# The mixer's output projection as seven block products, in a two-layer encoder trunk

## The chip, the cores and the metric

The kernel runs on one core of a Trainium2 chip, in one launch. The metric is the device time of one execution in microseconds, the lower the better. All arithmetic is float32 in accuracy: each float32 operand of a matmul is split into a high part, rounded by a copy to the type `F32R`, and a low part, the difference, and each product is three matmuls (high x high, high x low, low x high).

## The reference

Sequence 512, model width 1024, two layers. In each layer:

```
u = RMSNorm(h)
q_a,k_a,v_a, q_r,k_r,v_r,g_r, gate_a,gate_b = split(u @ w_in)
A = dilated attention(q_a,k_a,v_a);  B = silu(g_r) * GroupNorm(retention(q_r,k_r,v_r))
merged = sigmoid(gate_a) * (A @ w_att_out) + sigmoid(gate_b) * (B @ w_ret_out)
h = h + RMSNorm(merged @ w_out)                                  # the mixer's output projection
h = h + RMSNorm(relu(RMSNorm(h) @ w_up)^2 @ w_down)              # the MLP, 4096 wide
h = h + sigmoid(RMSNorm(h) @ w_ple_gate) * RMSNorm(p @ w_ple_proj)
```

The change concerns `merged @ w_out`, a product of 512 x 1024 by 1024 x 1024, and the read-out of `p @ w_ple_proj`.

## The kernel before

**Order of the work.** Only TensorE's (PE's) order is written out by hand. The instructions of the other engines and queues are ordered at build time by a scheduler, by priority and by when they are ready; what is wrapped in `soon` gets 300 steps of priority, so read-outs and norms go ahead of weight splits.

**Weights.** All weights come from one packed array in chunks of 128 x 1024, in the order of `PLAN_LAYER`. `ITEMS` lists what PE uses one after the other: a chunk, or a sum of chunks. `load` (L247) fetches chunks by an SP DMA into the ring `R` of four buffers; `total` (L260) makes a sum in a buffer of ring `X` (two buffers): an SP DMA fetches one chunk, and an accumulating DMA, issued by POOL, adds another. A "chain" adds a further chunk to the sum that product P5 left. `prefetch` (L271) makes the two parts of each item: ACT's copy (L278) for the high one, a subtraction on DVE or POOL (L301) for the low one, into one of five `wt` buffers. `chunk` (L289) asks for an item and runs up to three items ahead.

**Seven products in the MLP.** The down projection already runs six of its eight slices as block products of the Strassen-Winograd kind: `operands` (L826) forms differences of blocks of the activations, `total` differences and sums of weight blocks (signs are folded into additions and the read-outs), `product` (L843) runs one of the seven products, and `evac_prod` (L855) adds it up.

**Around the change.** For c in 0..7, `b_gate` and a matmul job on `ro` run on PE (24 matmuls each), DVE forms `m` (L751), and POOL adds it to `fb` (L752). `fb` holds `merged` transposed, two column groups to a tile. Its eight groups are split into the operand store `uT` (L755). Then `row_job` (L332) runs the output projection ("wo") as two halves of the columns: 96 matmuls for all four token blocks together, then 96 for one token block after the other. `evac_wo` (L761) reads a result out: ACT's sum of squares (L351), DVE's product with the gain (L766), and after the second half `pre_norm` (L393): root on POOL (L359, L361), update of the residual `h` (L773), sums of squares, root, normalised row `un` (L406). Its transposes (L413) and the split into `uT` (L416, L417) are put off by seven steps of PE work, or eight in what follows (`step`, `pending`).

Then "pp", the ple projection, takes 48 matmuls, its operands `phl` and two weight chunks whose low parts POOL makes (`POOL_MORE`); its read-outs alternate between ACT (L794) and DVE (L796). The first three chunks of the MLP's "up" run early, the columns of token blocks 0 and 1 first, then those of blocks 2 and 3 (L862 to L875).

PSUM has eight banks: `acc` (four), `s` (two) and `tp` (two), each a ring.

Of the kernel before, what the change touches and what calls it, by code (L numbers as in the profile page):

```python
# [28 lines left out]
PRIO = 300  # L29
POOL_MORE = [("pp",0),("pp",1)]  # L30
BG = 40
# [31 lines left out]
def _slot(e):  # L63
# [16 lines left out]
    + [("gb", c) for c in range(GB)] + [x for c in range(8) for x in ([("gb", c)] if c >= GB else []) + [("ro", c)]]  # L80
    + [("wo", c) for c in range(8)]
    + [("pp", c) for c in range(2)]
# [10 lines left out]
def _items():  # L93
    out = []
    for i in range(NL):
        for kind, c in PLAN_LAYER:
            e = 2 * (c // 8) + c % 4 // 2
            if kind == "up" and c >= 4 and c // 4 <= UNITS:
# [101 lines left out]
def block(ctx: ExitStack, tc: tile.TileContext, x, pT, w, dl, gains, cs, lc, rel, eye, out):  # L200
# [58 lines left out]

    def total(key, src):  # L260
        if src[0] == "chain":
            r = chain["sum"]
        else:
            r = blk("X", [P, D], name="wsum")
            nc.sync.dma_start(r, rows(src[0]))
            if key[1] == "P5":
                chain["sum"] = r
        nc.gpsimd.dma_start(r, rows(src[1]), accum_op=ALU.add)  # L268
        return r
# [369 lines left out]
    def one_layer(i, h):  # L639
# [106 lines left out]
        for c in range(8):  # L746
# [5 lines left out]
            nc.gpsimd.tensor_tensor(fb[c // 2][:, c % 2, :], m, fb[c // 2][:, c % 2, :], op=ALU.add)  # L752
        for c in range(8):
            src = fb[c // 2][:, c % 2, :]
            split(uT[:, :, c, :], src)  # L755
        g_post, g_pre = gain_row(5 * i + 1), gain_row(5 * i + 2)

        acc = [blk("V", [P, D], name="acc") for _ in range(NT)]
        ssq = [[None, None] for _ in range(NT)]

        def evac_wo(hf):  # L761
            @soon
            def f(t, ps):
                hs_ = HALVES[hf]
                ssq[t][hf] = sumsq(ps, t2("junk"), None if hf else 1e-6)
                nc.vector.tensor_tensor(acc[t][:, hs_], ps, g_post[:, hs_], op=ALU.mult)  # L766
                if hf:
                    pre_norm(h[t], t, g_pre, residual(t, acc, rstd_of(*ssq[t])))
            return f

# [4 lines left out]

        row_job([(i, "wo", c) for c in range(4)], u_lhs, evac_wo(0))
        row_job([(i, "wo", 4 + c) for c in range(4)], u_lhs, evac_wo(1), ONES)

# [7 lines left out]
        for hf in range(2):  # L786
            hsl = slice(hf * S, (hf + 1) * S)
            ch = chunk(i, "pp", hf)
            for t in range(NT):
                ps = bank(PP_BANKS[4 * hf + t])  # L790
                for k in range(2):
                    row_mm(ps, ch, k, lambda a, k, t: phl[k][:, a, t * P:(t + 1) * P], k, t, k == 0, k == 1)
                if t % 2:
                    nc.scalar.activation(pn[t][:, hsl], ps, AF.Copy)  # L794
                else:
                    nc.vector.tensor_copy(pn[t][:, hsl], ps)  # L796
                step(AGE_PP)
# [64 lines left out]
        early = []  # L862
        for j in range(2):
            settle(PAIRS[j])
            for c in range(EARLY):
                if not j:
                    early.append(bank(EARLY_BANKS[c]))
# [169 lines left out]
```

## Time and profile before

| | us |
|---|---|
| Time, median of 3 runs | 1796.14 (1793.64 to 1797.11) |
| Profiled execution, its own time | 1794.64 |
| Its span, first to last instruction | 1792.9 |
| Mean granted clock of TensorE | 1.0 of full speed |

| Engine | busy us | share |
|---|---|---|
| PE, matmuls | 1772.4 | 99% |
| PE, weight loads | 1466.2 | 82% |
| DVE | 1145.4 | 64% |
| ACT | 807.5 | 45% |
| POOL | 382.6 | 21% |

Busy time is the union of an engine's instructions in the profiled execution; the matmuls are pipelined, so that they overlap and their ends are modelled. The DMA queues moved 274.58 MB, 153 GB/s on average.

### The profile page before, as it was taken

Reading aid. Unit: us, or ns where it says so; the run is one execution under the profiler, and the core shown is the slowest. Engines: PE = TensorE matmul, PEld = TensorE weight load, DVE = VectorE, ACT = ScalarE, POOL = GpSimd, SP = SyncE. Lnnn points to the kernel's source line nnn. Section 1 sums busy time; section 2 is a strip of 40 time slices with the busy share of each in tenths; the row PEclk is TensorE's granted clock in tenths of the full one; section 3 lists DMA queues with packets and bytes.
Section 4 is the critical chain, followed back from the end, with each engine's and each line's share of the span. In section 5 each row is a group of like instructions: output and inputs, shape, how many; then the busy total and the mean of one; then the engine's idle time right before and its main releaser. Section 6 shows DMA issues by size and latency. Waiting matters only on the chain.

```text
span 1792.9 us, 22127 instructions
## 1 busy us (share of the span) xinstructions
PE 1772.4 (99%) x8209; PEld 1466.2 (82%) x8209; DVE 1145.4 (64%) x1803; ACT 807.5 (45%) x1271; POOL 382.6 (21%) x354
## 2 busy tenths in 40 slices
PE   8999999999999999999999999999999999999998
PEld 6888788888898888888788887888888888888887
DVE  6676777743465677674656767677444657667754
ACT  4255444332466454433443555444333664444342
POOL 2312244311142001002123222442012410000030
PEclk9999999999999999999999999999999999999999
DMA  5555464552347655552346545555422566664421
GB/s 213 194 193 159 149 212 137 166 175 95 117 142 188 165 158 161 156 184 70 129 141 214 165 145 172 184 159 187 136 101 99 165 170 156 169 175 130 165 71 60
DMA packets 87807, 274.58 MB, mean 153 GB/s; under 512 B 11921, under 2 KB 20497, under 8 KB 87698
## 3 DMA queue, kind: packets, MB, share of 16 engines
q1 hardware_dynamic: 80786, 247.99, 40.7%
q0 software_dynamic: 6912, 25.17, 8.3%
q8 instruction: 65, 1.06, 0.2%
q14 instruction: 44, 0.36, 0.1%
HBM read 239.55 MB, written 33.55 MB: 152 GB/s over the span
## 4 chain that ended last, share of the span: by engine, by line
PE 89%; DVE 4%; POOL 2%; ACT 2%; issue 1%; DMA 1%; SPq 0%; POOLq 0%; ACTq 0%
PE acc L312 28%; PE acc L322 19%; PE s L312 18%; PE acc L849 8%; PE tp L849 4%; PE tp L612 2%; PE tp L544 2%; PE tp L507 2%; PE acc L871 1%; PE tp L413 1%; POOL wt L301 1%; PE s L525 1%; PE s L526 1%; PE s L590 1%; PE s L871 1%
## 5 line engine op out<-in xcount | busy, mean ns | idle before, releaser
L312 PE MATMUL acc<-uT,wt 128*128 128x512 f32 x1920 | 472.8, 392 | 0.0
L312 PEld LDWEIGHTS acc<-uT,wt 128*128 128x128 f32 x1920 | 356.2, 188 | 71.8
L301 DVE TENSOR_TENSOR wt<-raw,wt 128x1024 fp32r<-128x1024 f32 x217 | 279.4, 1292 | 187.6 <-ACT wt L278 187.1
L278 ACT ACTIVATE wt<-raw 128x1024 fp32r<-128x1024 f32 x280 | 293.9, 1055 | 223.0 <-PE acc L312 114.0
L322 PE MATMUL acc<-wt,uT 128*128 128x512 f32 x1320 | 320.8, 396 | 4.4 <-ACT uT L416 1.8
L312 PE MATMUL s<-uT,wt 128*128 128x512 f32 x1392 | 323.7, 389 | 0.0
L312 PEld LDWEIGHTS s<-uT,wt 128*128 128x128 f32 x1392 | 261.1, 188 | 54.1
L322 PEld LDWEIGHTS acc<-wt,uT 128*128 128x128 f32 x1320 | 245.6, 189 | 55.6 <-DVE uT L417 2.6
L301 POOL TENSOR_TENSOR wt<-raw,wt 128x512 fp32r<-128x512 f32 x126 | 173.2, 1395 | 408.1 <-ACT wt L278 339.1
L849 PE MATMUL acc<-wt,op 128*128 128x512 f32 x672 | 159.5, 389 | 0.0
L849 PEld LDWEIGHTS acc<-wt,op 128*128 128x128 f32 x672 | 126.1, 188 | 26.2
L268 POOL DMA_DIRECT2D wsum<-in_w_dram x48 | 42.8, 900 | 420.1 <-DVE wt L301 141.0
L892 ACT ACTIVATE relu<-s 128x512 f32<-128x512 f32 x60 | 35.7, 595 | 180.7 <-PE s L312 172.0
L860 DVE TENSOR_TENSOR sumP<-acc,sumP 128x512 f32<-128x512 f32 x92 | 61.8, 686 | 56.4 <-PE acc L849 56.1
L312 PE MATMUL acc<-retT,wt 128*128 128x512 f32 x384 | 89.3, 389 | 0.0
L322 PE MATMUL acc<-wt,ff 128*128 128x512 f32 x384 | 88.5, 390 | 0.0
L301 DVE TENSOR_TENSOR wt<-wsum,wt 128x1024 fp32r<-128x1024 f32 x48 | 60.6, 1263 | 41.7 <-ACT wt L278 41.7
L312 PEld LDWEIGHTS acc<-retT,wt 128*128 128x128 f32 x384 | 72.1, 188 | 15.0
L322 PEld LDWEIGHTS acc<-wt,ff 128*128 128x128 f32 x384 | 71.8, 188 | 14.8
L304 ACT ACTIVATE rt<-rz 128x512 fp32r<-128x512 f32 x64 | 40.3, 631 | 91.5 <-DVE rz L594 91.0
L849 PE MATMUL tp<-wt,op 128*128 128x512 f32 x336 | 80.7, 389 | 0.0
L849 PEld LDWEIGHTS tp<-wt,op 128*128 128x128 f32 x336 | 63.1, 188 | 13.1
(165 smaller groups left out, 2153.5 us busy)
## 6 DMA issues: line engine op xcount, KB each, us to landing
raw<-in_w_dram SPq DMA_DIRECT2D x280, 512.0 KB, 3.7
wsum<-in_w_dram POOLq DMA_DIRECT2D x48, 512.0 KB, 5.5
kk<-stk SPq DMA_DIRECT2D x128, 128.0 KB, 3.8
wsum<-in_w_dram SPq DMA_DIRECT2D x24, 512.0 KB, 3.3
stq<-rr SPq DMA_DIRECT2D x16, 512.0 KB, 3.4
qs<-stq SPq DMA_DIRECT2D x128, 64.0 KB, 2.9
stk<-rr SPq DMA_DIRECT2D x16, 512.0 KB, 3.0
stv<-vr SPq DMA_DIRECT2D x16, 512.0 KB, 4.4
```

The source lines that it names most:

```text
L268: nc.gpsimd.dma_start(r, rows(src[1]), accum_op=ALU.add)
L278: nc.scalar.activation(t[:, 0, :], r, AF.Copy)
L301: eng.tensor_tensor(dst, src, hi.bitcast(F32), op=ALU.subtract)
L304: nc.scalar.activation(dst[:, 0], src, AF.Copy, scale=scale)
L312: nc.tensor.matmul(ps, lhsT=t[:, a, (off + k) * P:(off + k + 1) * P], rhs=r, start=k == 0 and n == 0, stop=k == kts - 1 and n == 2)
L322: nc.tensor.matmul(ps, lhsT=lhs(a, k, t), rhs=ch[:, b, j * S:(j + 1) * S], start=first and n == 0, stop=last and n == 2)
L507: nc.tensor.matmul(o, lhsT=v, rhs=pt[k][:, hl, :], start=k == 0 and hl == 0, stop=k == 3 and hl == 1)
L544: nc.tensor.transpose(ps[:, t * P:(t + 1) * P], zs[t][:, k * P:(k + 1) * P], ident)
L612: nc.tensor.matmul(o, lhsT=v[:, k, a * P:(a + 1) * P], rhs=rt[k][:, b, :], start=n == 0, stop=n == 11)
L849: nc.tensor.matmul(ps, lhsT=op[:, a, k, j * P:(j + 1) * P], rhs=t[:, b, k * S:(k + 1) * S], start=k == 0 and n == 0, stop=k == 1 and n == 2)
L860: nc.vector.tensor_tensor(a, ps, a, op=ALU.add)
L871: nc.tensor.matmul(early[c][:, 256 * j:256 * j + 256], lhsT=t[:, a, k * P:(k + 1) * P], rhs=uT[:, b, k, 256 * j:256 * j + 256], start=k == ...
```

## The change

`w_out` and `merged` are cut into two by two blocks: tokens in halves of 256, the inner dimension and the columns in halves of 512. Seven products P1 to P7 replace the eight block products; each has two weight items (q = 0, 1) of 12 matmuls. P5 and P7 use a sum of two weight chunks, P6 and P4 add one more chunk to P5's sum, which is held in ring `X`; P7's sum goes into ring `R`. The operands are differences of blocks of `fb`; P1, P5, P4 and P2 keep theirs in `uT`, the others in new tiles of ring `P`. The results of a product are read out by DVE additions into `acc`; P4 finishes token blocks 2 and 3, P2 blocks 0 and 1, and the early "up" takes blocks 2 and 3 first. Gain products of the right halves go to POOL. The low parts of pp's two weight chunks move from POOL to DVE, and its read-outs all go to ACT, with priority.

```diff
-POOL_MORE = [("pp",0),("pp",1)]
+POOL_MORE = []
...
-    + [("wo", c) for c in range(8)]
+    + [("wo", c) for c in (0, 1, 4, 5, 6, 7, 2, 3)]
...
+                if c == 0:
+                    b11, b21, b12, b22 = ([CHUNK[i, "wo", 2 * b + q] for q in range(2)] for b in range(4))
+                    out += [((i, "wo" + p, q), tuple(b if b == "chain" else b[q] for b in src)) for p, src in (
+                        ("P1", (b11,)), ("P5", (b11, b12)), ("P6", ("chain", b22)), ("P7", (b12, b22)),
+                        ("P3", (b22,)), ("P4", ("chain", b21)), ("P2", (b21,))) for q in range(2)]
+                continue
...
     def total(key, src):
+        at = key[2] if key[1][:2] == "wo" else "sum"
         if src[0] == "chain":
-            r = chain["sum"]
+            r = chain[at]
         else:
-            r = blk("X", [P, D], name="wsum")
+            held = key[1][-2:] == "P5"
+            r = blk("X" if held or at == "sum" else "R", [P, D], name="wsum")
             nc.sync.dma_start(r, rows(src[0]))
-            if key[1] == "P5":
-                chain["sum"] = r
+            if held:
+                chain[at] = r
         nc.gpsimd.dma_start(r, rows(src[1]), accum_op=ALU.add)
...
-        for c in range(8):
-            src = fb[c // 2][:, c % 2, :]
-            split(uT[:, :, c, :], src)
...
+        def wo_operand(x, q, src, at=None):
+            if at is None:
+                at = blk("P", [P, 2, 2, 256], F32R, name="wop")
+            nc.scalar.activation(at[:, 0], src, AF.Copy)
+            nc.vector.tensor_tensor(at[:, 1], src, at[:, 0].bitcast(F32), op=ALU.subtract)
+            wop[x, q] = at
...
+        def sum_x(q, o):
+            nc.vector.tensor_tensor(o, f2[q][:, :, 256:], f1[q][:, :, 256:], op=ALU.subtract)
+            return o
...
+        for q in range(2):
+            wo_operand("P1", q, f1[q][:, :, :256], lo_k[q][:, :, :, :256])
+        wx = sums(sum_x)
+        wy = sums(sum_y)
+        for q in range(2):
+            wo_operand("P5", q, wx[q], lo_k[q][:, :, :, 256:])
+            wo_operand("P6", q, wy[q])
+        wz = sums(sum_z)
+        for q in range(2):
+            wo_operand("P7", q, wz[q])
+        wv = sums(sum_v)
+        for q in range(2):
+            wo_operand("P3", q, wv[q])
+        for q in range(2):
+            wo_operand("P4", q, f2[q][:, :, 256:], hi_k[q][:, :, :, 256:])
+        for q in range(2):
+            wo_operand("P2", q, f2[q][:, :, :256], hi_k[q][:, :, :, :256])
...
+        def done_wo(t, hf, src, eng):
+            hs_ = HALVES[hf]
+            ssq[t][hf] = sumsq(src, t2("junk"), None if hf else 1e-6)
+            eng.tensor_tensor(acc[t][:, hs_], src, g_post[:, hs_], op=ALU.mult)
+            if not hf:
+                pre_norm(h[t], t, g_pre, residual(t, acc, rstd_of(*ssq[t])))
...
+        @soon
+        def evac_wo(x, j, ps):
+            (l1, r1), (l2, r2) = ([a[:, sl] for sl in HALVES] for a in (acc[j], acc[2 + j]))
+            if x == "P1":
+                nc.scalar.activation(l1, ps, AF.Copy)
+            elif x == "P5":
+                w5.append(ps)
+            elif x == "P6":
+                nc.vector.tensor_tensor(l2, ps, l1, op=add)
+                nc.vector.tensor_tensor(r1, w5[j], l2, op=add)
+            elif x == "P7":
+                nc.vector.scalar_tensor_tensor(r2, ps, -1.0, r1, op0=ALU.mult, op1=ALU.subtract)
+                nc.vector.tensor_tensor(l2, ps, l2, op=add)
+                done_wo(2 + j, 1, r2, nc.gpsimd)
+            elif x == "P3":
+                nc.vector.scalar_tensor_tensor(r1, ps, -1.0, r1, op0=ALU.mult, op1=ALU.subtract)
+                done_wo(j, 1, r1, nc.gpsimd)
+            elif x == "P4":
+                nc.vector.tensor_tensor(l2, ps, l2, op=add)
+                done_wo(2 + j, 0, l2, nc.vector)
+            else:
+                nc.vector.tensor_tensor(l1, ps, l1, op=add)
+                done_wo(j, 0, l1, nc.vector)
+
+        w5 = []
+        wo_banks = [bank(tag) for tag in ("acc", "acc", "s", "s", "acc", "acc")]
+        for m, pr in enumerate(("P1", "P5", "P6", "P7", "P3", "P4", "P2")):
+            pss = [wo_banks[(2 * m + j) % 6] for j in range(2)]
+            for q in range(2):
+                t = chunk(i, "wo" + pr, q)
+                for j in range(2):
+                    for k in range(2):
+                        for n, (a, b) in enumerate(HL):
+                            nc.tensor.matmul(pss[j], lhsT=wop[pr, q][:, a, k, j * P:(j + 1) * P], rhs=t[:, b, k * S:(k + 1) * S],
+                                             start=q == 0 and k == 0 and n == 0, stop=q == 1 and k == 1 and n == 2)
+                    if q:
+                        evac_wo(pr, j, pss[j])
+                    step()
...
-                if t % 2:
-                    nc.scalar.activation(pn[t][:, hsl], ps, AF.Copy)
-                else:
-                    nc.vector.tensor_copy(pn[t][:, hsl], ps)
+                soon(nc.scalar.activation)(pn[t][:, hsl], ps, AF.Copy)
...
-        for j in range(2):
+        for j in (1, 0):
             settle(PAIRS[j])
             for c in range(EARLY):
-                if not j:
+                if j:
                     early.append(bank(EARLY_BANKS[c]))
```

## Rows read from the trace of the kernel before

**Rows 1.** Page, part 1: engine, busy us (share of the span), instructions.

```profile
PE 1772.4 (99%) x8209; PEld 1466.2 (82%) x8209; DVE 1145.4 (64%) x1803; ACT 807.5 (45%) x1271; POOL 382.6 (21%) x354
```

**Rows 2.** Who waited for whom, PE alone: total us, times, longest; first and last of nine.

```profile
PE tp L544 <- DVE pt L301: 3.5, 2, 1.7
...
PE tp L413 <- DVE un L403: 0.7, 2, 0.3
```

**Rows 3.** Timeline of PE, layer 0, output projection to early up: start us, us, operation.

```profile
455.02 5.60 PE L312 MATMUL acc<-retT,wt 128*128 128x512 f32 x24
...
460.46 35.52 PE L322 MATMUL acc<-wt,uT 128*128 128x512 f32 x156
...
518.47 3.04 PE L871 MATMUL s<-uT,wt 128*128 128x256 f32 x24
...
527.11 3.04 PE L871 MATMUL s<-uT,wt 128*128 128x256 f32 x24
```

**Rows 4.** Line 322 in layer 0's output projection: min/median/max ns, first and last start.

```profile
L322 PE MATMUL acc<-wt,uT x192: 387/389/476, 460.5 to 505.6; 128*128 128x512 f32 x192
```

**Rows 5.** Windows: stretch and its length, busy us (instructions) by engine, PE clock, DMA share, GB/s.

```profile
460.50:482.20 21.70, 21.70 (x97) 17.99 (x96) 8.68 (x14) 6.95 (x11) 2.29 (x1) 1.00 0.31 106
482.20:505.80 23.60, 23.60 (x114) 19.68 (x113) 11.80 (x21) 12.23 (x28) 9.84 (x16) 1.00 0.24 90
505.80:518.50 12.70, 12.70 (x66) 10.69 (x65) 12.18 (x18) 7.90 (x16) 1.78 (x5) 1.00 0.70 248
518.50:535.75 17.25, 17.25 (x146) 17.25 (x145) 6.94 (x11) 8.52 (x14) 10.18 (x8) 1.00 0.32 98
...
633.70:677.20 43.50, 43.50 (x193) 36.03 (x192) 30.96 (x40) 20.56 (x27) 4.94 (x6) 1.00 0.63 161
...
1347.10:1405.10 58.00, 58.00 (x273) 48.38 (x272) 32.95 (x52) 27.29 (x55) 13.83 (x21) 1.00 0.37 131
```

**Rows 6.** Groups by line, forms apart: busy us, mean ns, idle before and releaser.

```profile
L278 ACT ACTIVATE wt<-raw 128x1024 fp32r<-128x1024 f32 x280 | 293.9, 1055 | 223.0 <-PE acc L312 114.0 <-PE acc L322 73.1 <-PE acc L849 16.5
...
L301 POOL TENSOR_TENSOR wt<-raw,wt 128x512 fp32r<-128x512 f32 x126 | 173.2, 1395 | 408.1 <-ACT wt L278 339.1 <-DMA kk<-stk 36.0 <-DVE rb L477 19.2
...
L935 POOL TENSOR_TENSOR sumP<-sumP,gain 128x512 f32<-128x512 f32 x8 | 12.1, 1536 | 136.8 <-ACT junk L351 136.8
```

**Rows 7.** Timeline of DVE, layer 0, before and through the output projection and pp.

```profile
450.88 2.12 DVE L301 TENSOR_TENSOR wt<-raw,wt 128x1024 fp32r<-128x1024 f32 x1 [0.34 <-ACT wt L278]
...
492.61 1.41 DVE L406 SCALAR_TENSOR_TENSOR un<-h,rstd,gain 128x512 f32<-128x512 f32 x2 [1.41 <-POOL rstd L361]
...
508.44 1.22 DVE L301 TENSOR_TENSOR wt<-raw,wt 128x1024 fp32r<-128x1024 f32 x1
509.58 0.68 DVE L766 TENSOR_TENSOR acc<-acc,gain 128x512 f32<-128x512 f32 x1
510.18 1.41 DVE L773 SCALAR_TENSOR_TENSOR h<-acc,rstd,h 128x512 f32<-128x512 f32 x2
...
513.78 1.42 DVE L406 SCALAR_TENSOR_TENSOR un<-h,rstd,gain 128x512 f32<-128x512 f32 x2 [0.40 <-POOL rstd L361]
515.12 1.28 DVE L417 TENSOR_TENSOR uT<-tp,uT 128x512 fp32r<-128x512 f32 x2
```

**Rows 8.** Page, part 6: DMA issues of the block sums, KB each, median us to landing.

```profile
wsum<-in_w_dram POOLq DMA_DIRECT2D x48, 512.0 KB, 5.5
...
wsum<-in_w_dram SPq DMA_DIRECT2D x24, 512.0 KB, 3.3
```

**Rows 9.** Timeline of ACT, layer 0: the first square sum of block 0.

```profile
487.86 0.60 ACT L351 ACTIVATE junk<-acc 128x512 f32<-128x512 f32 x1 [3.80 <-PE acc L322]
```

**Rows 10.** Timeline of POOL, layer 0: two additions of the gated branch.

```profile
450.62 1.29 POOL L752 TENSOR_TENSOR fT<-m,fT 128x512 f32<-128x512 f32 x1 [9.59 <-DVE m L751]
461.83 2.29 POOL L752 TENSOR_TENSOR fT<-m,fT 128x512 f32<-128x512 f32 x1 [9.92 <-DVE m L751]
```

More of the change, by code (lines that the diff above doesn't have):

```diff
@@ L97, in _items @@
             e = 2 * (c // 8) + c % 4 // 2
+            if kind == "wo":
+                if c == 0:
[4 more added lines that the diff above has]
+                continue
             if kind == "up" and c >= 4 and c // 4 <= UNITS:
@@ L752, in one_layer @@
             nc.gpsimd.tensor_tensor(fb[c // 2][:, c % 2, :], m, fb[c // 2][:, c % 2, :], op=ALU.add)
-        for c in range(8):
-            src = fb[c // 2][:, c % 2, :]
-            split(uT[:, :, c, :], src)
         g_post, g_pre = gain_row(5 * i + 1), gain_row(5 * i + 2)
+        wop = {}
+        def wo_operand(x, q, src, at=None):
[4 more added lines that the diff above has]
+            wop[x, q] = at
@@ new lines, in one_layer, with sums, sum_z @@
+        f1, f2 = fb[:2], fb[2:]
+        lo_k, hi_k = ([uT[:, :, 4 * kh + 2 * q:4 * kh + 2 * q + 2, :] for q in range(2)] for kh in range(2))
+        def sums(f):
+            return [f(q, t2("ws").rearrange("p (s n) -> p s n", s=2)) for q in range(2)]
+        def sum_x(q, o):
+            nc.vector.tensor_tensor(o, f2[q][:, :, 256:], f1[q][:, :, 256:], op=ALU.subtract)
+            return o
+        def sum_z(q, o):
+            nc.vector.tensor_tensor(o, f1[q][:, :, :256], f1[q][:, :, 256:], op=ALU.subtract)
+            return o
@@ new lines, in sum_y, with sum_v @@
+        def sum_y(q, o):
+            nc.vector.scalar_tensor_tensor(o, wx[q], -1.0, f1[q][:, :, :256], op0=ALU.mult, op1=ALU.subtract)
+            return o
+        def sum_v(q, o):
+            nc.vector.scalar_tensor_tensor(o, wy[q], -1.0, f2[q][:, :, :256], op0=ALU.mult, op1=ALU.subtract)
+            return o
+        for q in range(2):
[5 more added lines that the diff above has]
+            wo_operand("P6", q, wy[q])
@@ L758, in one_layer @@
+        wz = sums(sum_z)
[8 more added lines that the diff above has]
+            wo_operand("P2", q, f2[q][:, :, :256], hi_k[q][:, :, :, :256])
         acc = [blk("V", [P, D], name="acc") for _ in range(NT)]
         ssq = [[None, None] for _ in range(NT)]
[L761 to L769, printed above, removed]
+        LH, RH = HALVES
@@ L774, in residual @@
             return upd
-        row_job([(i, "wo", c) for c in range(4)], u_lhs, evac_wo(0))
-        row_job([(i, "wo", 4 + c) for c in range(4)], u_lhs, evac_wo(1), ONES)
+        def done_wo(t, hf, src, eng):
[4 more added lines that the diff above has]
+                pre_norm(h[t], t, g_pre, residual(t, acc, rstd_of(*ssq[t])))
+        add = ALU.add
```

## The prediction

> **What bounds the kernel now.** I read the busy shares first: TensorE (PE) is busy for 99% of the span, DVE for 64% [rows 1]. Busy time alone proves little, because matmuls overlap, so the list of PE's waits comes next: nine kinds of wait, 3.5 us for the largest and 0.7 us for the smallest, 15.6 us together in 1792.9 us [rows 2]. PE is fed almost without a gap. The time of this kernel is the number of its matmuls times their spacing, plus about 16 us.
>
> The third view is PE in order of time where the change is made. 24 matmuls of 512 columns stand from 455.02 to 460.46 us, so one costs 5.44/24 = 0.2267 us of PE; its own duration of 0.389 us is a pipelined one [rows 3, 4]. The mixer's output projection ("wo") starts at 460.46 with 192 matmuls, "pp" (the ple projection, 48 of them) ends at 518.47: 58.01 us for 240 x 0.2267 = 54.41 us of matmuls, so the four groups of transposes cost 0.9 us each and nothing is left over for a stall [rows 3]. In the windows of this stage, and in that of layer 1, PE is busy throughout [rows 5].
>
> The fourth view is the other engines in the same windows: DVE has 8.68 us of work in the first 21.7 us of wo, 11.80 in the next 23.6, 12.18 in 12.7 (pp), 6.94 in 17.25 (the early columns of "up") [rows 5]. DVE is half idle around wo and full during pp. That is where the change must be paid.
>
> Sums are made against the profiled execution: 1794.64 us, that is its span of 1792.9 and 1.74 around it, 1.5 below the median of 1796.14. A difference found in the span is applied to the median.
>
> **The change part by part.**
>
> *Matmuls.* Seven products of 24 replace 192 matmuls by 168: 24 fewer per layer, the same shape. 24 x 0.2267 = 5.44 us per layer, 10.88 us for two. This is the only gain, and all of it is on the path. By the matmuls' own durations (0.389 us) it would be 18.7 us. The Trainium skill ("Perfetto Trace Analysis", Identifying the Most-Contended Engine) says that busy time of matmuls misleads, pipelined ones being shown otherwise than they run; rows 3 and 4 agree, 0.389 against 0.2267, and the sum goes by the spacing.
>
> *Weights.* 14 items with 12 matmuls each (2.72 us) replace 8 with 24 (5.44 us). Each item costs ACT a copy of 1.06 us [rows 6] and DVE a split that occupies it for 1.14 us, from 508.44 to 509.58 [rows 7]: DVE +6.8 us, ACT +6.4 us per layer. An item needs 2.2 us of work each 2.72 us, on two engines, and five buffers let it run four items (10.9 us) ahead. The MLP stage already lives like this: 30.96 us of DVE work in 43.5 us with a full PE [rows 5]. So nothing on the path. SP issues 10 loads and POOL 8 accumulating ones per layer in place of 8 plain ones. Landing takes 3.3 and then 5.5 us [rows 8], together 8.8, less than the 10.9 us ahead; the first sums use buffers outside the ring, free once the retention heads are done, and can come much earlier. The DMA share is 0.31 and 0.24 here, and 0.70 was reached in pp [rows 5], so bandwidth is there. POOL waits for landings in its queue, and behind such a wait stand the additions of the gated branch and the reciprocal roots of the norm. Bounds 0 to 1 us per layer; I take 0.
>
> *Operands.* 14 splits and 8 sums replace 8 splits: 14 more DVE operations at 0.60 us (spacing from 509.58 to 510.18 [rows 7]) make 8.4 us, and six ACT copies of 0.6 us [rows 9]. P1 needs only the first half of the gated branch, done long before. The late operand is P5's second half: last "ro" matmul at 460.6, DVE product 0.69, POOL addition 1.29 to 2.29 [rows 10], DVE difference 0.69, ACT copy 0.6, DVE split 0.69: 464.6 to 465.6. PE reaches it after P1 and half of P5, at 460.46 + 8.16 = 468.6. Two weight splits in the way (2.3 us) would use up that cover; without it the cost is at most 1.5 us. I take 0.
>
> *Read-outs.* 14 PSUM additions on DVE (four each for P6 and P7, two each for P3, P4 and P2) are 8.4 us, of which the eight of P6 and P7 meet a DVE with room. Four gain products go from DVE to POOL, at 1.54 us each [rows 6]. A DVE weight split beside POOL's addition took 2.12 us, against 1.22 without [rows 7, 10]. The Trainium skill ("GPSIMD Engine Reference", 1. Specifications) has the reason: POOL shares its SBUF interfaces with DVE, where an instruction with two SBUF inputs contends. The trace agrees. By that rule the four products would take up to 4 x 1.54 x 0.9/1.29 = 4.3 us of DVE per layer, and 1798 in all if nothing covered it; I take the cover, since they fall under P7 and P3.
>
> *The ple projection.* POOL's four halves of low parts (1.40 us each [rows 6]) become two DVE splits, +2.3 us; four read-outs move to ACT, DVE -2.4, ACT +2.4. Near zero in sum, but all in the full stretch below.
>
> *The norms, moved together.* Before, the second half of wo finishes one token block each 5.44 us and its norm follows at once. Now blocks 2 and 3 finish with P4, 1.36 us apart, and blocks 0 and 1 with P2. One block needs of DVE: addition 0.60, gain 0.60, two updates 1.41, two normalised halves 1.34, two uT low parts 1.28, two small ones 0.30: 5.5 us [rows 7]. Four blocks are 22.1 us, with the five weight splits due then 27.8. PE's time from P4's first result to the second half of early "up" is 1.36 + 5.44 (P2) + 10.88 (pp) + 3.6 (transposes) + 8.64 (from 518.47 to 527.11 [rows 3]) = 29.9 us. DVE would be 93% full over that stretch; from 482.2 to 535.75 it is now 30.9 in 53.6 us, 58% [rows 5]. Here the stalls come, at two places:
> - The first pp group writes the PSUM bank that holds P2's first result, complete only 1.36 us before. Its addition waits on DVE behind the updates of blocks 2 and 3 (2.82 us) and perhaps a split (1.14): PE waits between 0 and 2.82 + 1.14 + 0.60 - 1.36 = 3.2 us. I take 1.5, half of it, because the order in the queue is open.
> - Transposes stand at fixed places in pp. Alone, a block took from 487.86 to 494.02 us, 6.2 us from its result to its normalised row [rows 7, 9], 6.9 with the new addition. Block 2 has 1.36 + 5.44 + 2.72 = 9.5 us, so 2.6 spare, and shares DVE with block 3; blocks 0 and 1 have 11.3 us. Bounds 0 to 2; I take 0.6.
>
> Early "up" begins with blocks 2 and 3, which are ready first; that order costs nothing itself.
>
> Sum: 2.1 us of stall per layer, 4.2 in two; 10.88 - 4.2 = 6.7 us gained, 1796.14 - 6.7 = 1789.4 us.
>
> **Rivals.**
> - *Nothing stalls:* 1796.14 - 10.88 = 1785.3 us. For it: PE stays full over the MLP products, which use the same pattern with 71% of DVE [rows 5]. Against: the 93% above.
> - *Given back:* each bound is met (3.2 + 2), 5.2 us per layer, and the time is 1795.7. For it: a serial norm with DVE full. Against: all of them have to fall unluckily in both layers.
> - *Slower, by DVE contention in pp:* the five splits of the stretch take 2.12 beside POOL's work (+0.98 each, 4.9 us), and four copies of 1.06 us on ACT delay the square sums (4.2), making 36.9 us of chain against 29.9, 7.0 per layer; with the bank 8.5. Two layers: 17.0 - 10.88 = 6.1 slower, 1802.3 us. It decides from 5.44 us per layer on. For it: the 2.12 us row. Against: POOL loses its low parts in pp and keeps mainly short roots there.
> - *The change does not do what it says:* fewer matmuls, but other stages shift with the new queue orders and lose a few us anywhere. This lands between the first two or at no change; it is counted with them.
>
> **How the numbers follow.** Forecast 0.50 (its own range 1786.5 to 1793), nothing stalls 0.20, given back 0.20, slower 0.10. A measurement of this kernel tells 0.2%, 3.6 us. Faster than 1792.5: nearly all of the first two and a little of the third, 0.70; within 0.2%: 0.20; slower: 0.10. Range: low 1784, the case without stalls less 1.3 for the spread of the runs; high 1796, the given-back case. Outside stay the slower case and small tails.
>
> **What would show it.** PE with 168 matmuls per layer at 0.2267 us in wo, about 39 us long. P5's second half without a wait. If I am right, PE's waits in these windows are new and stand at pp's first group (released by a DVE addition in PSUM) and at its transposes (released by DVE un), some 2 us per layer, with DVE over 85% busy from P4's end through pp. Wrong: waits of PE inside wo on weights or operands, or more than 5 us per layer at pp, or stalls in stages that the change does not touch.

## The result, and the profile after

Slower. Median 1826.24 us (1822.28 to 1827.60, four runs) against 1795.51 us for the kernel before in the same series; ratio 1.0174, 95% interval 1.0161 to 1.0186. Forecast were 1789.4 us, with 1784 to 1796 as the range. The profiled execution has a span of 1820.5 us, 27.6 more than before.

PE's busy time barely moved, and the other engines' grew. The first part of the page, which answers to [rows 1]:

```profile
PE 1774.1 (97%) x8161; PEld 1460.8 (80%) x8161; DVE 1197.2 (66%) x1859; ACT 831.2 (46%) x1307; POOL 404.9 (22%) x370
```

PE has 48 matmuls fewer, as forecast, and yet is busy longer: some of its matmuls ran at a lower clock. Its waits (who waited for whom; total us, times, longest) answer to [rows 2]:

```profile
PE tp L422 <- DVE un L415: 12.1, 7, 3.4
PE acc L331 <- ACT un L360: 5.5, 2, 3.3
PE tp L422 <- DVE uT L426: 5.3, 4, 1.5
...
PE s L865 <- DVE uT L771: 3.1, 2, 1.6
```

The first three are new in kind or size. They stand in pp (L331) and at its transposes (L422), which turn the normalised row `un` into `uT` through the PSUM bank `tp`; the last is P5's operand. The second names ACT's sum of squares, but pp's first group needs a PSUM bank that holds a result of P2. The DVE addition that reads this result (L853, 505.15 to 505.83 us in the view of DVE below) ends within 0.1 us of it. PE in order of time in layer 0 (start us, us, operation, idle before and its releaser), to be read beside [rows 3]:

```profile
461.41 5.60 PE L865 MATMUL acc<-wt,uT 128*128 128x512 f32 x24
467.94 0.73 PE L865 MATMUL s<-wt,uT 128*128 128x512 f32 x2 [0.93 <-ACT uT L770]
470.25 5.28 PE L865 MATMUL s<-wt,uT 128*128 128x512 f32 x22 [1.58 <-DVE uT L771]
...
479.21 8.23 PE L865 MATMUL acc<-wt,wop 128*128 128x512 f32 x35 [0.73 <-DVE wt L310]
...
492.72 11.04 PE L865 MATMUL acc<-wt,uT 128*128 128x512 f32 x48
505.98 3.36 PE L331 MATMUL acc<-wt,phl 128*128 128x512 f32 x12 [2.22 <-ACT un L360]
...
514.45 1.32 PE L422 MATMUL tp<-ident,un 128*128 128x128 f32 x8 [2.25 <-DVE un L415]
515.53 4.58 PE L331 MATMUL acc<-wt,phl 128*128 128x512 f32 x12
...
523.29 0.66 PE L422 MATMUL tp<-ident,un 128*128 128x128 f32 x4 [1.79 <-DVE un L415]
525.14 0.66 PE L422 MATMUL tp<-ident,un 128*128 128x128 f32 x4 [1.20 <-DVE un L415]
...
530.69 0.66 PE L422 MATMUL tp<-ident,un 128*128 128x128 f32 x4 [1.34 <-DVE uT L426]
...
532.58 3.03 PE L960 MATMUL s<-uT,wt 128*128 128x256 f32 x24
...
549.84 2.46 PE L321 MATMUL s<-uT,wt 128*128 128x512 f32 x10
```

Three stretches can be taken from it. The mixer's projection ("wo") runs from 461.41 to 503.70, 42.3 us, where 45.3 stood before (460.46 to 505.79, two groups of transposes in it). Pp with its transposes runs from 503.70 to 532.58, 28.9 us instead of 12.7. Early up takes 17.3 in both. So the layer loses 13.1 us from wo to early up (-3.04 + 16.20 - 0.02). Two of pp's four groups of transposes stood in wo before, 1.8 us. In layer 1 the same stretch, from wo to the full-width up products, went from 75.29 us (1347.11 to 1422.40) to 89.40 (1361.20 to 1450.60): +14.1. Together 27.25 of the 27.6 us: the rest of the kernel is as it was.

In windows (columns as in [rows 5]) the granted clock falls in pp, behind some of PE's pauses: 0.50 is the lower of the clock's two levels, 1.2 GHz, for the whole stretch. The 12 matmuls at 515.53 take 4.4 us to the next start where 2.7 is usual.

```profile
461.40:503.70 42.30, 39.06 (x169) 31.11 (x167) 39.71 (x48) 24.01 (x38) 14.44 (x11) 1.00 0.68 174
503.70:532.60 28.90, 19.63 (x82) 14.05 (x82) 23.16 (x40) 18.86 (x42) 8.66 (x17) 0.88 0.55 197
...
516.00:518.00 2.00, 2.00 (x6) 1.53 (x6) 1.57 (x3) 0.40 (x1) 0.40 (x1) 0.50 0.00 0
```

What PE waits for is in DVE's queue, in order of time (answering to [rows 7]). L310 is a weight split, L850 and L853 the read-outs of P4 and P2, L820 the update of the residual, L415 the normalised row:

```profile
494.39 5.69 DVE L310 TENSOR_TENSOR wt<-raw,wt 128x1024 fp32r<-128x1024 f32 x3
500.01 1.27 DVE L850 TENSOR_TENSOR acc<-acc,acc 128x512 f32<-128x512 f32 x2
...
505.15 0.68 DVE L853 TENSOR_TENSOR acc<-acc,acc 128x512 f32<-128x512 f32 x1
...
509.36 0.75 DVE L415 SCALAR_TENSOR_TENSOR un<-h,rstd,gain 128x512 f32<-128x512 f32 x1
...
524.34 0.74 DVE L415 SCALAR_TENSOR_TENSOR un<-h,rstd,gain 128x512 f32<-128x512 f32 x1
525.00 0.74 DVE L820 SCALAR_TENSOR_TENSOR h<-acc,rstd,h 128x512 f32<-128x512 f32 x1
525.67 0.14 DVE L362 TENSOR_SCALAR ss<-ss 128x1 f32<-128x1 f32 x1
525.73 0.68 DVE L426 TENSOR_TENSOR uT<-tp,uT 128x512 fp32r<-128x512 f32 x1
527.43 1.42 DVE L415 SCALAR_TENSOR_TENSOR un<-h,rstd,gain 128x512 f32<-128x512 f32 x2 [1.02 <-POOL rstd L370]
```

P4's first result is complete 18 matmuls behind its start, at 492.72 + 24 x 0.2267 - 1.36 = 496.8; DVE adds it at 500.01, behind three weight splits, and block 2's normalised row is ready at 510.1, 13.3 us after its product. P2's first result is complete at 502.2; block 0's row is ready at 525.1, 22.8 us after it.

The last view shows what changed around these results: DVE's groups (busy us, mean ns) in the 21.8 us that end with wo's last matmul, first of the kernel before (484.0 to 505.8 us, the three largest groups; they did not stand ahead of the prediction), then of the one after (481.9 to 503.7 us).

```profile
L773 DVE SCALAR_TENSOR_TENSOR h<-acc,rstd,h 128x512 f32<-128x512 f32 x6 | 4.2, 748 | 0.5 <-POOL rstd L361 0.4
L406 DVE SCALAR_TENSOR_TENSOR un<-h,rstd,gain 128x512 f32<-128x512 f32 x4 | 2.8, 748 | 2.8 <-POOL rstd L361 2.8
L766 DVE TENSOR_TENSOR acc<-acc,gain 128x512 f32<-128x512 f32 x3 | 2.1, 689 | 4.7 <-ACT junk L351 4.7
```

```profile
L310 DVE TENSOR_TENSOR wt<-raw,wt 128x1024 fp32r<-128x1024 f32 x7 | 11.6, 1687 | 0.0
L310 DVE TENSOR_TENSOR wt<-wsum,wt 128x1024 fp32r<-128x1024 f32 x2 | 2.4, 1216 | 0.0
```

Before, the updates of three row blocks and the normalised rows of two lay there, and no weight split at all: the right half of wo uses its four weights for one row block after the other (4 x 5.44 = 21.8 us), so nothing fresh is needed. After, nine splits lie there, 14.0 us of them, and not one update or normalised row.

### The profile page after: what moved, and what is told of

The parts are those of the page before. It is cut to its first block, busy times and chain, and to the rows that moved or that the text cites. A ratio compares the mean times of both kernels' runs of the same rounds, so it can differ in the third digit from the quotient of the medians.

```text
span 1820.5 us, 22228 instructions
## 1 busy us (share of the span) xinstructions
PE 1774.1 (97%) x8161; PEld 1460.8 (80%) x8161; DVE 1197.2 (66%) x1859; ACT 831.2 (46%) x1307; POOL 404.9 (22%) x370
## 4 chain that ended last, share of the span: by engine, by line
PE 82%; DVE 6%; ACT 3%; POOL 3%; DMA 2%; issue 2%; SPq 0%; POOLq 0%; ACTq 0%; DVEq 0%
PE acc L321 26%; PE s L321 17%; PE acc L331 14%; PE acc L938 8%; PE tp L938 4%; PE tp L621 2%; PE tp L553 2%; PE tp L516 1%; PE acc L960 1%; DMA wsum<-in_w_dram 1%; DVE wt L310 1%; PE acc L865 1%; POOL rstd L370 1%; POOL wt L310 1%; ACT un L360 1%
## 5 line engine op out<-in xcount | busy, mean ns | idle before, releaser
L310 DVE TENSOR_TENSOR wt<-raw,wt 128x1024 fp32r<-128x1024 f32 x217 | 284.9, 1320 | 173.1 <-ACT wt L287 172.6
L287 ACT ACTIVATE wt<-raw 128x1024 fp32r<-128x1024 f32 x276 | 289.8, 1054 | 207.2 <-PE acc L321 105.9
L310 POOL TENSOR_TENSOR wt<-raw,wt 128x512 fp32r<-128x512 f32 x118 | 162.1, 1395 | 366.5 <-ACT wt L287 287.0
L331 PE MATMUL acc<-wt,uT 128*128 128x512 f32 x936 | 232.3, 398 | 5.2 <-ACT uT L425 2.6
L331 PEld LDWEIGHTS acc<-wt,uT 128*128 128x128 f32 x936 | 173.8, 190 | 41.6 <-ACT uT L425 3.0
L277 POOL DMA_DIRECT2D wsum<-in_w_dram x64 | 57.3, 898 | 470.8 <-DVE wt L310 152.8
L310 DVE TENSOR_TENSOR wt<-wsum,wt 128x1024 fp32r<-128x1024 f32 x64 | 81.9, 1287 | 41.2 <-ACT wt L287 41.0
L287 ACT ACTIVATE wt<-wsum 128x1024 fp32r<-128x1024 f32 x64 | 67.6, 1056 | 67.3 <-DMA wsum<-in_w_dram 33.8
L331 PE MATMUL acc<-wt,ff 128*128 128x512 f32 x384 | 88.5, 390 | 0.0
L331 PEld LDWEIGHTS acc<-wt,ff 128*128 128x128 f32 x384 | 71.8, 188 | 14.8
```

Of the source, the lines that this page charges most:

```text
L287: nc.scalar.activation(t[:, 0, :], r, AF.Copy)
L310: eng.tensor_tensor(dst, src, hi.bitcast(F32), op=ALU.subtract)
L331: nc.tensor.matmul(ps, lhsT=lhs(a, k, t), rhs=ch[:, b, j * S:(j + 1) * S], start=first and n == 0, stop=last and n == 2)
```

## The experiments

Each time is a median; the ratio is to the kernel before in the same series, with its 95% interval (the change itself: 1.0174). Unless said otherwise a run is the changed kernel with one edit.

**Undoing one part at a time.** The gain products back on DVE:

```diff
-                done_wo(2 + j, 1, r2, nc.gpsimd)     # and the same for block j
+                done_wo(2 + j, 1, r2, nc.vector)
```

> The changed kernel with one edit: the four gain products of the right halves back on DVE instead of POOL. Theory G (the products on POOL and the weight splits on DVE slow each other just before the read-out of P4: the four products took 2.2 us each, the splits beside them 2.3, and the first addition of P4 began 3.2 us after its matmuls): the addition then begins within 1 us of the matmuls, the norms move forward by 3 us in each layer, and the time falls from 1826 to about 1818. Theory N (two norms at once are too slow for transposes that stand at fixed places in pp, whatever starts them): the chain starts up to 3 us earlier but remains late; 1820 to 1824. Theory B (the PSUM bank) and theory Q (the added load of pp on DVE and ACT): no change, 1826.

1835.39 us, 1.0228 [1.0212, 1.0243]: 9 us slower than the change. P4's first addition then came 1.1 us behind its product (498.50 against 497.4) instead of 3.2, about as theory G expected, and yet PE's wait for pp's first bank grew to 6.4 us. The products on GpSimd do delay the read-out, but moving them to DVE, which then has four products more, gains nothing.

Transposes five steps later in pp and early up:

```diff
-AGE_PP = 8
+AGE_PP = 13
```

> The changed kernel with one number changed: transposes of the four blocks wait for 13 steps of PE work in pp and early up instead of 8, so blocks 2 and 3 come near the end of pp and blocks 0 and 1 inside early up. Theory N (the places of the transposes on PE are too early for norms that come two at a time): PE goes through pp without pauses, the granted clock stays at 1.00, and most of the 14 us per layer lost in pp returns: about 1800 to 1804. Theories G and B: the first pp group still waits (2.2 and 3.3 us) and the norms are as late; the wait moves to early up: 1815 or more. Theory Q (DVE and ACT are short of time in pp): the wait moves to the end of pp and little is won, 1820.

1836.28 us, 1.0233 [1.0218, 1.0249]. The waits at the transposes shrink, and a greater one takes their place:

```profile
PE acc L331 <- ACT pn L391: 20.9, 2, 10.4
```

Pp's read-outs now stand behind the norms' squares in ACT's queue, and pp's second use of a bank waits for them.

Other banks for pp:

```diff
-PP_BANKS = ("acc", "acc", "s", "acc", "acc", "s", "acc", "acc")
+PP_BANKS = ("s", "s", "acc", "acc", "acc", "acc", "s", "s")
```

> The changed kernel with another order of PSUM banks for the eight groups of pp: the first two groups use banks that P3 held, not those of the results of P2. Theory B (the start of pp waits for DVE to read the results of P2): the wait of 2.2 and 3.3 us at the first group goes, 1826 falls to about 1820. Theory N: the wait at the first group goes too but comes back at the transposes of block 2, two groups later, for which the norm is no earlier: 1825 to 1827. Theories G and Q: as theory N.

1827.24 us, 1.0184 [1.0169, 1.0199]: no gain. The wait at pp's first group is gone, and returns at the transposes (15.6 us instead of 12.1 on DVE's un).

Pp's low parts and read-outs as before:

```diff
-POOL_MORE = []
+POOL_MORE = [("pp",0),("pp",1)]     # and pn alternating between ACT and DVE
```

> The changed kernel with pp as before the change: low parts of its two weight chunks on POOL, its read-outs alternating between ACT and DVE without priority. Theory Q (the load that the change puts on DVE and ACT in pp delays the norms): DVE loses 2.3 us of splits per layer and gets 2.4 of read-outs, ACT loses 2.4; if this load matters 1815 to 1820. Theory N: no gain, 1824 to 1830; the roots of the norm on POOL stand behind its low parts, so rather a loss of 1 to 3 us per layer.

1828.69 us, 1.0192 [1.0175, 1.0209]. No gain; PE's wait for pp's first bank grew to 6.2 us here too. In e2 and e3, where a wait was removed, it came back at the next thing that the same late norm feeds.

**Rings and weights.** Norms with their own one-column scratch for each row block (e5); own ring for the operand sums x and y, and phl, the operands of pp, split later, at 485.31 us instead of 463.06 (e6); both (e7; the edit to phl is left out here):

```diff
-        return sm.tile([P, n], F32, name=name, tag=f"c{n}")
+        if n == 1 and own[0] is not None:
+            return own[0].pop(0)            # 8 columns for each row block
...
-        wx = sums(sum_x)
-        wy = sums(sum_y)
+        wx = sums(sum_x, True)              # tag "g", four buffers
+        wy = sums(sum_y, True)
```

> The changed kernel with one edit: the one-column scratch tiles of the norms of the four token blocks (sums of squares, reciprocal roots) come from a tile of their own for each block, and not from the common ring of 24 columns. No arithmetic differs. Theory R (the ring of columns is handed out in the order of the program, so that the square sum of block 3 stands behind the whole norm of block 2 in the queue of ACT, that of block 0 behind block 3, and four norms of 6.2 us run one after the other): blocks 2 and 3 now overlap, and blocks 0 and 1, the last normalised row comes some 10 us earlier, PE waits in pp fall from about 11 us per layer to below 4, the clock stays up, and the time is 1800 to 1810. Theory N (the engines are too slow for two norms at once, whatever the order): nothing changes, 1823 to 1828. Theory G (gain products on POOL): the start of the chain is as late as before, 1820 to 1826.

> The changed kernel with the operands of the products alone put right: the sums x and y in a ring of their own (four buffers), so that the first sum can be formed before the last ro product, and the operands of pp (phl) in a buffer that is free only after P6, so that their splits do not stand ahead of the last ro product on DVE. The common ring of columns stays. Theory P (P5 waits 3 to 4 us per layer because DVE does the phl splits first, and the first sum only after the last ro product): the waits at P5 fall below 1.5 us per layer, 1826 goes to about 1820. Theory R says the same of P5 and that all waits in pp stay. If P5 alone drove the later lateness, more than 10 us would come back: 1815 or less.

> Both edits: own columns for the norms of each block, own ring for the sums x and y, phl later. If theories R and P hold and add up: 1826 less 16 to 26 for the norms and less 6 for P5, 1794 to 1804. If theory N holds: 1818 to 1822.

e5 took 1825.17 us, 1.0175 [1.0158, 1.0191]; e6 1826.12, 1.0183 [1.0162, 1.0204]; e7 1823.46, 1.0163 [1.0148, 1.0178]. In e6 P5's waits are gone, 2.5 us in layer 0 (P6's grew from 0.73 to 1.54), and the time is the same: PE comes earlier to pp and waits 5.7 us there, where it was 2.2 and 3.3. A wait ahead of a later one on the same chain costs nothing.

P7's weight sums out of the ring of raw weights (e8); that with e5's scratch and e6's ring for the sums (e9); e9 with the gain products on DVE (e11):

```diff
-            r = blk("X" if held or at == "sum" else "R", [P, D], name="wsum")
+            r = blk("X" if held or at == "sum" else "A", [P, D], name="wsum")
```

> The weight sums of the seventh block product (P7) lie in the ring of eight blocks that is empty at this time, so that the ring of four raw blocks holds raw weights alone. Nothing else is changed. Theory W (late weights): SP's queue no longer stands for the 23 us behind a raw load that waits for P7's sum, the raw loads are spread, their landing falls from 6.4 us to about 3.3, ScalarE's copies and VectorE's splits of weights come early and no longer stand ahead of the read-outs of P4; its first addition follows its product within 1.5 us where it took 3.2. The time falls from 1826 to 1805 to 1815 us. Theory N (the norm's chain of two row blocks is simply longer than the products of the ple projection cover): the queue is smooth, but transposes in the ple projection go on waiting for VectorE's norm about 6 us a layer, and the time stays within 3 us of 1824.

> As the run with P7's weight sums in the empty ring, and besides: own one-column scratch for the norms of each row block, and an own ring of four for the operand sums x and y, which were shown to remove the waits of P5. Theory W: with the weights early and both other orders gone, PE's waits in the ple projection fall below 3 us a layer, the granted clock stays near 1.0 there, and the time is 1788 to 1800 us. Theory N: P5's waits go (3 us a layer), the rest stays, 1820 us.

> As the run before it, with the four gain products of the mixer's read-outs on VectorE in place of GpSimd. Theory G2 (VectorE's splits are slowed by GpSimd's long products beside them and hold the read-outs): about 1 us a layer faster than the run before it. Theory W alone: VectorE is what the norms wait for, and four more products on it make it 1 to 3 us a layer slower, as this edit alone did (9 us in all).

e8 took 1823.85 us, 1.0163 [1.0148, 1.0178]; e9 1817.75, 1.0128 [1.0111, 1.0145]; e11 1827.50, 1.0179 [1.0162, 1.0196]. Half of theory W fell: P7's sum is not what holds up SP's queue, for in e8 its longest stand behind DVE's splits was 26.6 us, not less than the 23.1 of the change. So e8 did not make the weights early, and what early weights would give it does not show. e9 gave 8 us, the most of any version that computes all, and more than its parts gave alone, which was not explained; it is still 24 us behind the kernel before.

**When the row blocks are finished.** The kernel before, with its right half computed chunk by chunk, so that all four row blocks end in the last 5.4 us:

```diff
-        row_job([(i, "wo", 4 + c) for c in range(4)], u_lhs, evac_wo(1), ONES)
+        row_job([(i, "wo", 4 + c) for c in range(4)], u_lhs, evac_wo(1))
```

> The kernel before, with one edit: the right half of the mixer's output projection computes all four row blocks chunk by chunk, as its left half does, instead of block after block. The same matmuls, the same weights, nothing of the block products. All four row blocks are then finished in the last 5.4 us. Theory F: the norms stand bare behind the projection, PE waits in the ple projection and the clock falls there, 8 to 16 us a layer: 1810 to 1826 us. Theory W (the cost comes with the weight sums and VectorE's load of operands): 1794 to 1800 us.

1815.17 us, 1.0123 [1.0106, 1.0140]: 21 us slower, with not one block product in wo. PE in layer 0:

```profile
502.64 1.52 PE L322 MATMUL acc<-wt,phl 128*128 128x512 f32 x6
504.96 1.67 PE L322 MATMUL acc<-wt,phl 128*128 128x512 f32 x6 [0.80 <-DVE acc L766]
...
510.20 1.68 PE L322 MATMUL acc<-wt,phl 128*128 128x512 f32 x6 [2.18 <-DVE acc L766]
...
516.48 2.92 PE L322 MATMUL acc<-wt,phl 128*128 128x512 f32 x6 [3.73 <-DVE acc L766]
...
527.14 3.04 PE L871 MATMUL s<-uT,wt 128*128 128x256 f32 x24
```

The same picture as after the change: pp waits for a bank that the late norm reads, the group behind a pause runs slowly (2.92 for 1.68), and early up starts late. Pp takes 24.5 us (502.64 to 527.14), all four groups of transposes in it, with two weight splits on DVE in that time (506.87 and 513.14), where the kernel before has three. So a late finish is dear without the change's load on DVE.

Then the finish was moved forward in the changed kernel. P4 ahead of P3 (e12); besides, P3 and P2 row block by row block (e13); that with e9's edits (e14); that with P7 and P4 row block by row block too, the cadence of the kernel before (e17):

```diff
-        enumerate(("P1", "P5", "P6", "P7", "P3", "P4", "P2"))
+        enumerate(("P1", "P5", "P6", "P7", "P4", "P3", "P2"))
...
+        for j in range(2):
+            for m, pr in ((5, "P3"), (6, "P2")):
+                for q in range(2):
+                    wo_mm(pr, q, j, ...)
```

> The fourth product (P4) is computed ahead of the third (P3), with its operands and weights, so that row blocks 2 and 3 are finished 10.9 us ahead of the projection's end instead of 5.4. The same work, otherwise nothing changed. Theory F (the norms of all four row blocks now start at the projection's end, where before three of four lay under its matmuls): the norms of blocks 2 and 3 get 5.4 us more of cover; PE's waits in the ple projection fall by 2 to 4 us a layer and the clock drops less; 1826 becomes 1808 to 1818 us. Theory W (late weights and the splits in the queues): the weights and the order of the splits are about the same, so the time stays within 4 us of 1826.

> As the run before it, and the last two products (P3 and P2) are computed row block by row block: P3 and P2 for block 0, then P3 and P2 for block 1. The row blocks are then finished 13.6, 10.9, 5.4 and 0 us ahead of the projection's end; in the kernel before it was 16.3, 10.9, 5.4 and 0. Theory F: the norms lie under the products almost as in the kernel before, PE's waits in the ple projection fall below 3 us a layer and the granted clock stays near 1.0 there; what is left over the forecast are P5's operand waits of 3 us a layer: 1794 to 1804 us. Theory W: no change, 1820 to 1830 us.

> As the run before it, with the three smaller edits that were run together on the changed kernel and gave 8 us there (P7's weight sums in the empty ring, own ring for the operand sums x and y, own one-column scratch for the norms of each row block). Theory F: P5's waits go too, 1786 to 1796 us. Theory W: as those edits alone, 1812 to 1820 us.

> The run with all small edits (e14), and now the last four products go row block by row block: P7 and P4 for block 2, P7 and P4 for block 3, P3 and P2 for block 0, P3 and P2 for block 1. Each row block is finished 5.4 us after the one before it, 16.3, 10.9, 5.4 and 0 us ahead of the projection's end, the cadence of the kernel before; VectorE's whole load of the change is kept. Theory F in its sharper form (not only how late the last block is, but that two blocks at a time put their norms into the same in-order queues, so that the transposes of one stand behind the residual of the next): PE waits from the projection to the early up products fall from some 16 us a layer to under 5, the clock stays near 1.0, and the time is 1788 to 1802 us. Theory D (VectorE's load of 64 of 75 us): the cadence doesn't matter, 1808 to 1820 us.

e12 took 1829.16 us, 1.0196 [1.0174, 1.0218]; e13 1825.04, 1.0175 [1.0159, 1.0190]; e14 1818.10, 1.0133 [1.0117, 1.0148]; e17 1827.03, 1.0182 [1.0168, 1.0196]. All missed what theory F expected: nothing came back (e14's 8 us are those of e9). Yet in e13 and e14 pp itself recovered. In e14 it takes 13.3 us in layer 0 (518.33 to 531.58), two groups of transposes in it, where the kernel before took 12.7. The waits had moved into wo, to the transposes of the blocks that now stand there:

```profile
502.15 1.97 PE L426 MATMUL tp<-ident,un 128*128 128x128 f32 x8 [4.46 <-DVE un L419]
...
513.59 1.11 PE L426 MATMUL tp<-ident,un 128*128 128x128 f32 x4 [6.43 <-DVE bc L366]
...
518.33 1.31 PE L335 MATMUL acc<-wt,phl 128*128 128x512 f32 x5
...
531.58 3.04 PE L980 MATMUL s<-uT,wt 128*128 128x256 f32 x24
```

In e17, in the same layer, a wait for weights joins them:

```profile
494.58 2.50 PE L869 MATMUL acc<-wt,wop 128*128 128x512 f32 x5 [3.24 <-DVE bc L366]
...
503.73 2.93 PE L869 MATMUL acc<-wt,uT 128*128 128x512 f32 x6 [4.51 <-DVE wt L314]
...
520.81 2.92 PE L335 MATMUL acc<-wt,phl 128*128 128x512 f32 x6 [4.60 <-DVE acc L861]
```

The norms start earlier, and P2's weights wait for them (503.73): in DVE's queue P2's first split stands behind the update of block 3 and the transposed copies of block 2 (start us, us, operation):

```profile
498.40 1.42 DVE L824 SCALAR_TENSOR_TENSOR h<-acc,bc,h 128x512 f32<-128x512 f32 x2 [0.72 <-POOL bc L374]
...
501.58 2.09 DVE L314 TENSOR_TENSOR wt<-raw,wt 128x1024 fp32r<-128x1024 f32 x1
504.39 1.41 DVE L419 SCALAR_TENSOR_TENSOR un<-h,bc,gain 128x512 f32<-128x512 f32 x2 [0.71 <-POOL bc L374]
505.72 2.35 DVE L314 TENSOR_TENSOR wt<-raw,wt 128x1024 fp32r<-128x1024 f32 x2
```

**How much of it is DVE's load.** The changed kernel (e15), and e14 (e16), without the low parts of wo's operands and weights, so that wo's result is only roughly the reference's, from as many matmuls; and (b2) the kernel before with the low parts of its wo weights computed three times:

```diff
-            nc.vector.tensor_tensor(at[:, 1], src, at[:, 0].bitcast(F32), op=ALU.subtract)
...
-    nc.tensor.matmul(pss[j], lhsT=wop[pr, q][:, a, ...], rhs=t[:, b, ...], ...)
+    nc.tensor.matmul(pss[j], lhsT=wop[pr, q][:, 0, ...], rhs=t[:, 0, ...], ...)
```

> The changed kernel without the low parts of the mixer projection's operands and weights (14 subtractions of 0.68 us and 14 of 1.2 us or more a layer, about 27 us of VectorE); the high parts stand in their place, so that the matmuls are the same in number and form, and the projection's result is only roughly that of the reference. Theory D (VectorE is full from the projection to the early up products, 64 of 75 us, and read-outs and norms stand in its queue behind splits): most of the 31 us come back, 1790 to 1802 us. Theory F (the norms start at the end, whatever VectorE's load): their chain is shorter only by the queue, 1810 to 1820 us.

> The run with all small edits and the row blocks finished one after another (e14), and without the same low parts. Theories D and F together: neither a full VectorE nor a late finish is left, PE's waits in the projection and in the ple projection fall below 3 us a layer, and the time comes to what was forecast, 1783 to 1793 us. If a third cause is there (weights that come late, the queues' written order), it stays above 1800.

> The kernel before, with the low part of each of the mixer projection's eight weights computed three times over (16 more subtractions of 1.2 us a layer, 20 us of VectorE, about what the change adds there); the row blocks are finished as before. Theory D alone: VectorE's load is enough, 1802 to 1815 us. Theory D with F (the load hurts only where the norms start late): 1794 to 1799 us.

e15 took 1810.46 us, 1.0087 [1.0069, 1.0105]; e16 1805.83, 1.0064 [1.0046, 1.0082]; b2 1793.82, 0.9998 [0.9988, 1.0007]. DVE had 33.31 us of work instead of 20.48 in wo of b2 and nothing happened: its extra work came early, where DVE idled, and the norms' stretch was left alone. In e15 half of the loss came back (1.74% to 0.87%, 15.6 us). DVE has room in its wo, and pp is nearly as long as after the change:

```profile
458.70:497.40 38.70, 38.46 (x169) 31.29 (x168) 22.29 (x31) 25.25 (x39) 11.10 (x11) 1.00 0.82 220
497.40:524.80 27.40, 18.73 (x82) 13.69 (x82) 21.69 (x38) 17.91 (x41) 8.73 (x16) 0.88 0.43 160
```

27.4 us with an undisturbed wo (38.7 us, 168 x 0.2267 = 38.1): the norms' own chain behind wo, with nothing late ahead of it. Most of what came back did not come back in pp. The profiled executions of the change and of e15 differ by 13.6 us: 6.3 lie in the two layers' wo, 4.6 in their pp, and 2.7 ahead of layer 0's wo, nearly all of it in the first 34 us, where the two kernels are written alike. e16 has early blocks and a light DVE, and stays 11.5 us behind the kernel before: PE stands 6.5 us a layer at block 3's transposes, for which block 2's transposed copies must leave the two banks, and these stand in DVE's queue behind block 0's update.

```profile
504.27 2.37 PE L428 MATMUL tp<-ident,un 128*128 128x128 f32 x8 [6.51 <-DVE uT L432]
```

## Why the prediction was wrong

*Matmuls.* Right: 168 a layer at 0.2267 us (P4 and P2, 48 of them, go from 492.72 to 503.70 us). The -10.88 us are there. The trace shows a matmul longer than what it costs, 0.389 us against 0.2267, so the spacing was the measure to take.

*Norms: the step that failed.* The forecast put 2.1 us of stall on a layer, all of it here. Measured were 18.6 us in layer 0 (13.1 slower where 5.44 were to be gained) and 19.6 in layer 1. Of these 4.2 and 3.3 us lie in wo, and 14.4 and 16.3 in pp, counted against 48 x 0.2267 us and four groups of transposes at 0.9. The first term, pp's first group, "I take 1.5", was mis-sized: PE waited 2.22 and 3.29 us, about the upper bound of 3.2. The second, the transposes, "I take 0.6" with 2 as its bound, is where the forecast broke: PE waited 7.0 and 7.5 us there. The places were right; the spare time was not. Two errors lie in it. The spare time was worked out from a block's chain *alone*, 6.2 us, with 0.7 for the addition; two blocks that finish 1.36 us apart share DVE, ACT and POOL at every hand-over, and 13.3 and 22.8 us stand there, where 9.5 and 11.3 were allowed. And the stalls were judged by DVE's sum of busy time, 93%, as if what fits into the stretch were also on time. DVE was busy for 23.2 of pp's 28.9 us, 80%, and idle for the rest while PE waited, because a norm passes from engine to engine through queues of fixed order. A sum of busy times bounds a chain from below only. The prediction's own sign of being wrong, more than 5 us a layer at pp, is what came.

*Weights, "I take 0".* PE's wait on a weight in wo was 0.73 us a layer, so the bound of 1 held. One premise did not: the sum has four items of run-ahead (10.9 us), where `chunk` asks for three, 8.2 us, less than the 8.8 of the two landings. And the term looked only at PE's waits. The splits sit in DVE's queue ahead of P4's and P2's read-outs, in a stretch where there had been none, and put the norms' start off by 3.2 us. e15 prices the low parts at 15.6 us in all, by the profiles more of it in wo than in pp; how much of that is the splits and how much the operands' was not separated.

*Operands, "I take 0".* 0.93 + 1.58 us in layer 0, outside the bound of 1.5 (1.57 in layer 1), and without effect on the time, as e6 shows.

*Read-outs.* The cover by P7 and P3 did not hold: GpSimd's four products ran from 489.88 to 499.00 us, under P3 and P4. Three splits took 5.69 us beside them, just ahead of P4's read-out. Undoing that alone made it worse (e1).

*The clock* was in no term. In pp of layer 0 it cost about 1.7 us at 515.53 and 1.2 at 525.73, both behind waits.

*Rivals.* "Slower, by DVE contention in pp" named the direction and the place, with a tenth of the chance and 8.5 us a layer, less than half of what came. Its mechanism did not come: the four splits from 501.21 us on that lie in pp or just ahead of it took 1.2 us each, not 2.12. The slow ones stand in wo.

What the runs settle: a late finish of all row blocks costs 21 us in the kernel before, without any block product in wo (b1). In the changed kernel the stalls of both layers from wo to early up are 38.1 us, some 31 of them in pp. Without the low parts (e15) 27.2 stay, 26 of them in pp. So most of the loss is the norms' chain behind wo, and the low parts' load on DVE is the smaller part there. Outside the norms' stretch such a load cost nothing (b2). What the parts of that chain cost, the order of the queues and the pairing of the blocks, was not separated.

Not settled is whether any order of the queues brings the seven products out ahead: the kernel before keeps four weights for four row blocks at the end, and block products need fresh ones up to the last; no run here had both early blocks and no splits among the norms with all low parts computed. None of the versions beat the kernel before.

## What to carry to other kernels

Before work is cut from a stage, look at what the stage covers: list the engines' groups in its last 20 us, and ask which of them need its *last* results. An algorithm with fewer matmuls that finishes its outputs late and together can cost more than it saves, when a serial step across several engines follows each output. Here a row-by-row order over weights that stay was worth more (21 us) than the matmuls saved (10.9).

And where removing a wait doesn't move the time, look for the same chain's next wait before looking for another cause.

## What the runs showed of the hardware

PE's granted clock fell to 0.50 and 0.67 from 516 to 520 us, behind pauses of 2.22, 0.39 and 2.25 us, and to 0.54 and 0.61 from 526 to 530, behind 1.79 and 1.20; every window of the kernel before from 460 to 560 us has 1.00. Not each such pause did it: behind the first one of 2.22 us the clock was 1.00 (506 to 512 us), and in e15 also behind pauses of 0.54, 0.38 and 2.25 us (508 to 512). In pp of layer 0 the slow matmuls cost 2.9 us beside 9.2 us of waits.

GpSimd's 128x512 product and DVE's 128x1024 split slowed each other: 2.28 us each for two gain products (489.88 to 494.44 us), where [rows 6] have 1.54, and 1.9 us for a split beside them, where three others took 3.48 together:

```profile
489.88 4.56 POOL L826 TENSOR_TENSOR acc<-acc,gain 128x512 f32<-128x512 f32 x2 [9.18 <-ACT junk L360]
494.99 4.01 POOL L826 TENSOR_TENSOR acc<-acc,gain 128x512 f32<-128x512 f32 x2
```

```profile
477.94 3.48 DVE L310 TENSOR_TENSOR wt<-wsum,wt 128x1024 fp32r<-128x1024 f32 x3
```

The Trainium skill ("GPSIMD Engine Reference", 1. Specifications) says that the two share SBUF interfaces; the trace agrees, and adds that both sides pay.
